# Decay exponents from running sums by head, and half of the xbc low parts by adding transfers

## The chip, the cores and the metric

The kernel runs on one core of one Trainium2 chip. The metric is device microseconds for one execution, the median of several runs. The program is written in Python against a tile framework: the framework allocates tiles from pools, sets the semaphores, and fixes one order of instructions for each engine when the program is built. The engines are PE (TensorE, matrix products into PSUM banks), DVE (VectorE), ACT (ScalarE), POOL (GpSimd) and SP (SyncE, which here only issues transfers). Each engine works through its own queue in order.

## The reference

One encoder block on 256 tokens of width 2048, all in float32. The part that matters here is the mixer:

```python
proj = rmsnorm(h, mix_norm_pre) @ w_in          # z (1024), xbc (1536), dt (32), u (1024)
xbc = silu(dwconv_centred(xbc, conv_w, conv_b)) # 5 taps over tokens
xs, bm, cm = split(xbc)                         # 16 heads of 64; 2 groups of state 128
dt = softplus(dt_raw + dt_bias); a = -exp(a_log)
# for each direction, chunk of 128 tokens and head:
acum  = cumsum(dt * a)
decay = exp(where(causal, acum[l] - acum[s], -inf))
y_diag = einsum(C B^T, decay, x * dt)           # + a term that crosses the chunks
```

Both directions run over the same tokens; the backward one is the forward one on flipped arrays. After the mixer come the pooling mixer, the shared output projection, a gated conv-MLP of width 5632 and a per-layer embedding. The change touches only `decay` and the way in which the xbc columns of `w_in` are prepared.

## The kernel before

**Products in two parts.** TensorE works on a rounded float32 form (called fp32r in the profile). To keep float32 accuracy the kernel splits every operand into a high part (rounded to that form) and a low part (the rest), and adds three products: high by high, high by low, low by high. `split` (lines 138 to 149) does this for weights: ACT copies 1024 columns into `...h` (L147), and DVE subtracts that from the source into `...l` (L148). The high and the low tiles rotate through five buffers each, the loaded slabs (`raw`, 1024 KB each, issued by SP) through three.

**Stages.** First the columns for dt and u (`dtu`, until 52.5 us), then three slabs of xbc (`xbc2`, `xbc0`, `xbc1` in this order, each 512 columns through `feature_major`), then z, then the output projection and the rest, which the change leaves alone. In `feature_major` (lines 268 to 283) a slab has four loads u; each load is split in two halves j, and each half feeds 24 matmuls of 256 columns. After a slab come the row scale (`xr`, L356), the convolution (ACT for the middle tap, L367, and 16 DVE instructions for the others, L373), and tanh and a product for silu.

**Work aside.** After every u, `aside()` takes the next list out of `work` and issues its jobs; so the attention-like work of the mixer lies between the xbc blocks. Which jobs stand in which list is written by hand (lines 623 to 656). The framework's own order may move a job's instructions a little among the neighbouring ones.

**The decays.** For each chunk t and group q of four heads (eight in all), `seg_prep` builds a 128 x 2048 page on POOL: the high and the low part of dt * a, each times a triangular mask, for both directions (four products, L509). `seg` then runs four matmuls of 512 columns against `m_gt` and `m_lt`, which add up the exponents over the steps between s and l for both directions in one PSUM bank, and ACT takes the exponential out of PSUM into `E` (L518). `weigh` multiplies `E` by C B^T and dt (POOL L581, DVE L586 and L590).

**Banks.** PSUM has six main banks and two `misc` banks. All the jobs aside (`pool_mix`, `decays`, `seg`, `pool_map`, `cb`, `xs_turn`, `mix`) take `misc` banks in turn, so a job's first matmul waits until the one two places earlier has been read out. `pool_map` is read out by ACT (`cath`, L183) and DVE (`catl`, L184).

Of the kernel before, what the change touches and what calls it, by code (L numbers as in the profile page):

```python
# [21 lines left out]
H = 16  # L22
# [29 lines left out]
def build(nc, a, out):  # L52
# [5 lines left out]
    with tile.TileContext(nc) as tc, \  # L58
# [8 lines left out]
        def ins(r):  # L67
            return getattr(r, "ins", r)

        def page(name, dtype=F32):  # L70
            return gp.tile([P, 2048], dtype, tag="pg", bufs=13, name=name)
# [10 lines left out]
        def misc(name):  # L82
            return pc.tile([P, 512], F32, tag="misc", name=name)

        def mm(o, lhsT, rhs, start, stop):
            nc.tensor.matmul(o, lhsT, rhs, start=start, stop=stop, skip_group_check=True)  # L86


        ep = early.enter_context(tc.tile_pool(name="early", bufs=1))
# [18 lines left out]

        xt = [ep.tile([P, V_SCW + L], F32, name="xt0")] + [page(f"xt{i}") for i in (1, 2)]
        vt = cp.tile([P, V_N - V_SCW], F32, name="vt")  # L110
        small = ep.tile([P, 80 + 512], F32, name="small")

        last = {}

# [12 lines left out]

        last["dma"] = load(xt[0], a["x_cols"][:, :V_SCW + L])
        dtb, alog, dsk = small[:, :32], small[:, 32:64], small[:, 64:80]
        mask = small[:, 80:].rearrange("p (m f) -> p m f", m=4)  # L130

        def vec(i):
            return xt[0][:, i:i + 1] if i < V_SCW else vt[:, i - V_SCW:i - V_SCW + 1]
# [2 lines left out]
        spare = {}  # L136

        def split(name, src, nel, cuts=()):

            if name in spare:  # L140
                hi, lo = spare.pop(name)
            else:
                hi = wp.tile([P, 1056], F32R, tag="whi", bufs=5, name=f"{name}h")
                lo = wp.tile([P, 1056], F32R, tag="wlo", bufs=5, name=f"{name}l")
            for c0, c1 in zip((0, *cuts), (*cuts, nel)):
                s = slice(c0, c1)
                last["act"] = ins(nc.scalar.copy(hi[:, s], src[:, s]))  # L147
                last["dve"] = ins(nc.vector.tensor_sub(lo[:, s], src[:, s], hi[:, s].bitcast(F32)))  # L148
            return hi, lo

        def raw(name, src, a_, b_):
# [116 lines left out]
        def feature_major(name, w, c0, get, acc):  # L268

            for u in range(4):  # L270
                r = raw(f"{name}r{u}", w[u * 512:(u + 1) * 512, c0:c0 + 512]
                        .rearrange("(k p) c -> p k c", p=P), 4, 512)
                for j in range(2):
                    wh, wl = split(f"{name}{u}_{j}", r[:, j * 1024:(j + 1) * 1024], 1024)
                    for kk in range(2):
                        k = 4 * u + 2 * j + kk
                        xh, xl = get(k)
                        for f in range(4):
                            s = slice(kk * 512 + f * P, kk * 512 + (f + 1) * P)
# [108 lines left out]
        for u in range(0, NK, 2):  # L388
            r = [wp.tile([P, 2048], F32, tag="raw", bufs=3, name=f"dtur{u}") if u else r0, page(f"dtur{u + 1}")]
            for j in range(2):  # L390
                k = u + j
# [35 lines left out]
        with tc.issue_after(half[0]), tc.issue_after(half[1]):  # L427
            xs_ = [page(f"x{t}") for t in range(2)]
            for t in range(2):
                load(xs_[t], x[t * P:(t + 1) * P, :])  # L430
            rx = row_rstd("rx", xs_)
            m_gt, m_lt = (ep.tile([P, P], F32R, name=n) for n in ("m_gt", "m_lt"))
            nc.vector.tensor_copy(m_gt, mask[:, 2, :])
            nc.vector.tensor_copy(m_lt, mask[:, 3, :])
            aneg = ep.tile([P, 32], F32, name="aneg")
            nc.scalar.activation(aneg, alog, AF.Exp)
            nc.gpsimd.tensor_scalar(aneg, aneg, -1.0, None, op0=ALU.mult)


            pt = page("pt")[:, :512].rearrange("p (k t) -> p k t", k=2)  # L440
            load(pt, a["p_t"])
            pth = cp.tile([P, 2, L], F32R, name="pth")
            ptl = cp.tile([P, 2, L], F32R, name="ptl")
            nc.scalar.copy(pth, pt)
            nc.vector.tensor_sub(ptl, pt, pth.bitcast(F32))
# [10 lines left out]
        for t in range(2):  # L456
# [3 lines left out]
                                    op0=ALU.mult)  # L460
# [17 lines left out]
        nc.vector.tensor_scalar(e3, e3, 2.0, None, op0=ALU.mult)  # L478
        nc.vector.scalar_tensor_tensor(dtf, dtf, 0.0, e3, op0=ALU.max, op1=ALU.add)
        da = ep.tile([P, 2, 32], F32, name="da")  # L480
        dah = ep.tile([P, 2, 32], F32R, name="dah")
        dal = ep.tile([P, 2, 32], F32, name="dal")
        nc.vector.tensor_tensor(da, dt, aneg.unsqueeze(1).to_broadcast([P, 2, 32]), op=ALU.mult)
        nc.vector.tensor_copy(dah, da)
        nc.vector.tensor_sub(dal, da, dah.bitcast(F32))

# [10 lines left out]
                nc.gpsimd.tensor_mul(dec[:, d, :], dec[:, d, :], dt[:, d, d * H:(d + 1) * H])  # L497


        ee = [page(f"E{t}") for t in range(2)]  # L500
        steps = {}

        def seg_prep(i):
            t, q = divmod(i, 4)
            ap_ = page(f"ap{i}", F32R).rearrange("p (a h l) -> p a h l", a=4, h=4)
            for j in range(4):
                d, src = j // 2, (dah.bitcast(F32), dal)[j % 2]
                hs = slice(d * H + 4 * q, d * H + 4 * q + 4)
                nc.gpsimd.tensor_tensor(ap_[:, j], src[:, t, hs].unsqueeze(2).to_broadcast([P, 4, P]),  # L509
                                        mask[:, d, :].unsqueeze(1).to_broadcast([P, 4, P]), op=ALU.mult)  # L510
            steps[i] = ap_

        def seg(i):
            t, q = divmod(i, 4)
            sps, ap_ = misc(f"seg{i}"), steps.pop(i)
            for j in range(4):
                mm(sps, (m_gt, m_lt)[j // 2], ap_[:, j].rearrange("p h l -> p (h l)"), j == 0, j == 3)
            nc.scalar.activation(ee[t][:, q * 512:(q + 1) * 512], sps, AF.Exp)  # L518


        cat = Panel.__new__(Panel)
# [97 lines left out]
        def job(f, *args):  # L619
            return lambda: f(*args)  # L620

        xd = {}
        work.extend([
            [job(seg_prep, 0)],
            [job(seg_prep, 1), job(pool_mix, 0), job(pool_mix, 1)],
            [job(seg_prep, 2), job(pool_mix, 2), job(pool_mix, 3), job(decays)],
            [job(seg_prep, 3), job(seg, 0)],
        ])
        bc = xbc(2)
        work.extend([  # L630
            [job(seg_prep, 4), job(seg, 1), job(pool_map, 0), job(pool_map, 1)],
            [job(seg_prep, 5), job(seg, 2), job(cb, bc, 0), job(cb, bc, 1)],
            [job(seg_prep, 6), job(seg, 3), job(pool_map, 2), job(pool_map, 3)],
            [job(seg_prep, 7), job(seg, 4), job(weigh, 0, 0)],
        ])
        xa = xbc(0)
        work.extend([
            [job(seg, 5), job(weigh, 0, 1)],
            [job(seg, 6), job(xs_turn, xa, 0)],
            [job(seg, 7), job(weigh, 1, 0)],  # L640
            [job(weigh, 1, 1)],
        ])
        xb = xbc(1)
# [21 lines left out]
        for t in range(2):  # L665
# [13 lines left out]
            r = rms(f"yn{t}", [ss], rz[t][:, 1:2], n=2)  # L679
# [65 lines left out]
        h = [page(f"h{t}") for t in range(2)]  # L745
# [118 lines left out]
        for half in range(2):  # L864
# [35 lines left out]
def laid_out(a):  # L900

    def cols(*vs):
        return np.concatenate([v.reshape(-1, P).T for v in vs], axis=1)

    return {
        "x_cols": np.concatenate([cols(a["mix_norm_pre"][0]),
                                  a["x"][0].T.reshape(NK, P, L).transpose(1, 0, 2).reshape(P, NK * L)], axis=1),
        "p_t": a["p"][0, 0].T.reshape(2, P, L).transpose(1, 0, 2),
        "columns": np.concatenate([
            cols(a["ssd_conv_w"][0], a["ssd_conv_b"][0], a["ssd_norm"][0], a["pool_scale"][0], a["ffn_norm_pre"][0],  # L910
                 a["ffn_conv_w"][0], a["ple_norm_pre"][0], a["ffn_conv_b"][0]),
            np.broadcast_to(np.concatenate([a[n][0].reshape(-1) for n in ("ssd_dt_bias", "ssd_a_log", "ssd_d")]),
                            (P, 80)),
            masks().transpose(1, 0, 2).reshape(P, 4 * P)], axis=1),
    }


def masks():
    j = np.arange(P)[:, None]
    l = np.arange(P)[None, :]  # L920
    return np.stack([j <= l, j >= l, j > l, j < l]).astype(np.float32)


def constants():
# [17 lines left out]
```

## Time and profile before

| | |
|---|---|
| median of 3 runs | 1146.65 us (1146.38 to 1147.10) |
| the profiled execution | 1147.28 us |
| its span | 1145.5 us |
| TensorE busy | 1126.3 us (98%) |
| VectorE, ScalarE, POOL busy | 824.8, 598.3, 122.5 us |
| granted TensorE clock, mean | 0.994 |

The profile comes from one execution. "Busy" is the time in which an engine had an instruction under way. The granted clock says what share of full speed TensorE was allowed; 1.00 is full. A chain is followed back from the last instruction, at each step to what released it. A wait names the engine and line that waited and the one whose end let it go. Rows that group instructions give the count, the busy time in all and the mean duration; rows of a timeline give the start, the length and the instruction. L numbers are lines of the kernel.

### The profile page before, as it was taken

Reading aid. Unit: us, or ns where it says so; the run is one execution under the profiler, and the core shown is the slowest. Engines: PE = TensorE matmul, PEld = TensorE weight load, DVE = VectorE, ACT = ScalarE, POOL = GpSimd, SP = SyncE. Lnnn points to the kernel's source line nnn. Section 1 sums busy time; section 2 is a strip of 40 time slices with the busy share of each in tenths; the row PEclk is TensorE's granted clock in tenths of the full one; section 3 lists DMA queues with packets and bytes.
Section 4 is the critical chain, followed back from the end, with each engine's and each line's share of the span. In section 5 each row is a group of like instructions: output and inputs, shape, how many; then the busy total and the mean of one; then the engine's idle time right before and its main releaser. Section 6 shows DMA issues by size and latency. Waiting matters only on the chain.

```text
span 1145.5 us, 15408 instructions
## 1 busy us (share of the span) xinstructions
PE 1126.3 (98%) x6057; PEld 971.6 (85%) x6057; DVE 824.8 (72%) x1060; ACT 598.3 (52%) x812; POOL 122.5 (11%) x123
## 2 busy tenths in 40 slices
PE   9998999999999999999999999999999999999996
PEld 9997987888888888888888888888888888887885
DVE  6578896654777665666766766668888888898573
ACT  7533543553675454544544545545555556657462
POOL 0274504200110000000000000000000000002001
PEclk9998999999999999999999999999999999999998
DMA  9952347546365555555555565556466646564752
GB/s 358 337 184 74 111 150 267 201 156 216 121 213 186 192 192 195 190 185 184 184 187 193 181 207 189 184 184 221 159 209 221 204 163 221 187 206 159 226 179 74
DMA packets 129592, 219.03 MB, mean 191 GB/s; under 512 B 3696, under 2 KB 96752, under 8 KB 128624
## 3 DMA queue, kind: packets, MB, share of 16 engines
q1 hardware_dynamic: 129232, 217.70, 57.4%
q8 instruction: 47, 0.77, 0.3%
q10 hardware_dynamic: 288, 0.36, 0.1%
q14 instruction: 25, 0.20, 0.1%
HBM read 215.95 MB, written 2.10 MB: 190 GB/s over the span
## 4 chain that ended last, share of the span: by engine, by line
PE 92%; DVE 5%; POOL 1%; ACT 1%; issue 1%; POOLq 0%; DVEq 0%; ACTq 0%
PE va L86 21%; PE ga L86 21%; PE dna L86 17%; PE woa L86 8%; PE gt L86 7%; PE dtu L86 4%; PE z L86 4%; PE xbc L86 3%; PE dns L86 3%; DVE cv L373 2%; DVE w L586 1%; DVE xb_0l L148 1%; PE ple L86 1%; PE yd L86 0%; DVE h L726 0%
## 5 line engine op out<-in xcount | busy, mean ns | idle before, releaser
L86 PE MATMUL ga<-wox,ug_0h 128*128 128x512 f32 x352 | 125.5, 395 | 0.0
L86 PE MATMUL ga<-wox,ug_1h 128*128 128x512 f32 x352 | 125.1, 394 | 0.0
L86 PE MATMUL va<-wox,uv_0h 128*128 128x512 f32 x352 | 124.8, 393 | 0.0
L86 PE MATMUL va<-wox,uv_1h 128*128 128x512 f32 x352 | 124.8, 393 | 0.0
L86 PE MATMUL ga<-wox,ug_0l 128*128 128x256 f32 x352 | 99.1, 282 | 0.0
L86 PE MATMUL ga<-wox,ug_1l 128*128 128x256 f32 x352 | 99.1, 282 | 0.0
L86 PE MATMUL va<-wox,uv_0l 128*128 128x256 f32 x352 | 99.1, 281 | 0.0
L86 PE MATMUL va<-wox,uv_1l 128*128 128x256 f32 x352 | 99.1, 281 | 0.0
L86 PEld LDWEIGHTS va<-wox,uv_0h 128*128 128x128 f32 x352 | 66.1, 188 | 15.0
L86 PEld LDWEIGHTS va<-wox,uv_1h 128*128 128x128 f32 x352 | 66.1, 188 | 15.0
L86 PEld LDWEIGHTS ga<-wox,ug_1h 128*128 128x128 f32 x352 | 66.1, 188 | 14.9
L86 PEld LDWEIGHTS ga<-wox,ug_0h 128*128 128x128 f32 x352 | 66.1, 188 | 14.8
L86 PE MATMUL dna<-dn_0h,hs 128*128 128x512 f32 x248 | 75.8, 393 | 0.0
L86 PE MATMUL dna<-dn_1h,hs 128*128 128x512 f32 x248 | 75.6, 393 | 0.0
L767 POOL TENSOR_TENSOR fc<-fc,rfb 128x1024 f32<-128x1024 f32 x11 | 26.4, 2404 | 440.2 <-ACT fc L766 440.2
L86 PEld LDWEIGHTS ga<-wox,ug_0l 128*128 128x128 f32 x352 | 66.2, 188 | 0.1
L86 PEld LDWEIGHTS ga<-wox,ug_1l 128*128 128x128 f32 x352 | 66.2, 188 | 0.0
L86 PEld LDWEIGHTS va<-wox,uv_0l 128*128 128x128 f32 x352 | 66.2, 188 | 0.0
L86 PEld LDWEIGHTS va<-wox,uv_1l 128*128 128x128 f32 x352 | 66.2, 188 | 0.0
L86 PEld LDWEIGHTS dna<-dn_1h,hs 128*128 128x128 f32 x248 | 46.5, 188 | 10.8
L86 PEld LDWEIGHTS dna<-dn_0h,hs 128*128 128x128 f32 x248 | 46.5, 188 | 10.7
L86 PE MATMUL dna<-dn_0l,hs 128*128 128x512 f32 x124 | 40.2, 393 | 0.0
(1075 smaller groups left out, 2860.3 us busy)
## 6 DMA issues: line engine op xcount, KB each, us to landing
dn0r<-w_ffn_down SPq DMA_DIRECT2D x22, 1024.0 KB, 5.5
dn1r<-w_ffn_down SPq DMA_DIRECT2D x22, 1024.0 KB, 5.5
zr<-w_in SPq DMA_DIRECT2D x8, 1024.0 KB, 5.2
wo0r<-w_out SPq DMA_DIRECT2D x8, 1024.0 KB, 5.6
wo1r<-w_out SPq DMA_DIRECT2D x8, 1024.0 KB, 5.5
gt0r<-w_ple_gate SPq DMA_DIRECT2D x8, 1024.0 KB, 6.0
gt1r<-w_ple_gate SPq DMA_DIRECT2D x8, 1024.0 KB, 5.6
dtur<-w_in SPq DMA_DIRECT2D x14, 528.0 KB, 8.6
```

Source lines behind the costliest of these rows:

```text
L86: nc.tensor.matmul(o, lhsT, rhs, start=start, stop=stop, skip_group_check=True)
L148: last["dve"] = ins(nc.vector.tensor_sub(lo[:, s], src[:, s], hi[:, s].bitcast(F32)))
L373: nc.vector.scalar_tensor_tensor(o[:, lo:hi], i[:, lo + d:hi + d], vec(wcol + j * wstep + f), o[:, lo:hi], op0=ALU.mult, op1=ALU.add)
L586: nc.vector.scalar_tensor_tensor(w[:, h * P:(h + 1) * P], cbm[:, 0, g, t, :], dt[:, t, 8 * g + h:8 * g + h + 1], w[:, h * P:(h + 1) * P], ...
L767: nc.gpsimd.tensor_tensor(cv.rearrange("p (f t) -> p f t", f=4), cv.rearrange("p (f t) -> p f t", f=4), rfb.unsqueeze(1).to_broadcast([P, ...
```

## The change

**Exponents.** `seg_prep` is gone. The new `seg_sums`, once, computes running sums by matmul: for each chunk and direction, `da4` (dt * a, four copies by head, the sign turned for the backward direction) against a mask gives c[l] for all 16 heads in 64 rows, 16 heads in four blocks. It splits c into high and low, and spreads it by ACT over two pages: `seg_x` holds c[l] in rows 0 to 31 (high, low) and selectors in rows 32 to 63; `seg_w` holds negated selectors and c[s] so that a single matmul over 64 rows gives c[l] - c[s] for four heads. The selector halves are filled earlier, in the dtu stage (eight ACT instructions). `seg` is now one matmul of 512 columns for each direction, into two `misc` banks; ACT copies the first out, DVE takes the minimum with the second (the direction in which the pair is causal has the smaller exponent), and ACT takes the exponential in place.

**Low parts.** In `feature_major` the second half (j = 1) of each load now goes through `split_far`: ACT writes the negated slab, rounded, to the low tile; POOL issues a transfer that reads the same 512 KB of `w_in` from device memory again and adds it to that tile; ACT writes the high tile. So DVE has no part in it. There are 12 of these.

**Order.** The jobs aside are dealt anew: `seg_sums` goes into the third list, `seg` runs from the fourth on (two at first, then one each), and `cb` moves two lists later. The constants of `small` grow by nine columns.

```diff
+        low, among, four = small[:64, 592:593], small[:64, 593:597], small[:64, 597:601]
...
+        def split_far(name, src, far, nel):
...
+            nc.scalar.activation(lo[:, :nel], src[:, :nel], AF.Copy, scale=-1.0)
+            o = lo[:, :nel]
+            if len(far.shape) == 3:
+                o = o.rearrange("p (k c) -> p k c", k=far.shape[1])
+            nc.gpsimd.dma_start(o, far, accum_op=ALU.add)
+            nc.scalar.copy(hi[:, :nel], src[:, :nel])
+            return hi, lo
...
-                    wh, wl = split(f"{name}{u}_{j}", r[:, j * 1024:(j + 1) * 1024], 1024)
+                    piece = r[:, j * 1024:(j + 1) * 1024]
+                    if j:
+                        wh, wl = split_far(f"{name}{u}_{j}", piece, w[u * 512 + 256:(u + 1) * 512, c0:c0 + 512]
+                                           .rearrange("(k p) c -> p k c", p=P), 1024)
+                    else:
+                        wh, wl = split(f"{name}{u}_{j}", piece, 1024)
...
-            m_gt, m_lt = (ep.tile([P, P], F32R, name=n) for n in ("m_gt", "m_lt"))
-            nc.vector.tensor_copy(m_gt, mask[:, 2, :])
-            nc.vector.tensor_copy(m_lt, mask[:, 3, :])
+            seg_w = page("seg_w", F32R)[:64, :].rearrange("p (a q s) -> p a q s", a=4, q=4)
+            seg_x = page("seg_x", F32R)[:64, :].rearrange("p (a i l) -> p a i l", a=4, i=4)
+            for a_ in range(4):
+                nc.scalar.activation(seg_w[:32, a_], four[:32].unsqueeze(2).to_broadcast([32, 4, P]), AF.Copy,
+                                     scale=-1.0)
+                nc.scalar.copy(seg_x[32:, a_], among[32:].unsqueeze(2).to_broadcast([32, 4, P]))
...
-        dah = ep.tile([P, 2, 32], F32R, name="dah")
-        dal = ep.tile([P, 2, 32], F32, name="dal")
+        da4 = ep.tile([P, 2, 2, 4, H], F32, name="da4")
...
-        nc.vector.tensor_copy(dah, da)
-        nc.vector.tensor_sub(dal, da, dah.bitcast(F32))
+        for d in range(2):
+            nc.vector.tensor_scalar(da4[:, :, d], da[:, :, d * H:(d + 1) * H].unsqueeze(2).to_broadcast([P, 2, 4, H]),
+                                    1.0 - 2.0 * d, None, op0=ALU.mult)
...
-        def seg_prep(i):
...
-                nc.gpsimd.tensor_tensor(ap_[:, j], src[:, t, hs].unsqueeze(2).to_broadcast([P, 4, P]),
-                                        mask[:, d, :].unsqueeze(1).to_broadcast([P, 4, P]), op=ALU.mult)
+        def seg_sums():
+            cps = misc("cps")
+            for a_ in range(4):
+                mm(cps[:64, a_ * P:(a_ + 1) * P], da4[:, a_ // 2, a_ % 2].rearrange("p r h -> p (r h)"),
+                   mask[:, 3 * (a_ % 2), :], True, True)
+            hi, c = page("seg_h", F32R)[:64, :512], page("seg_c")[:64, :512]
+            nc.scalar.copy(hi, cps[:64, :])
+            nc.vector.scalar_tensor_tensor(c, hi.bitcast(F32), low, cps[:64, :], op0=ALU.mult, op1=ALU.add)
+            c4 = c.rearrange("p (a l) -> p a l", a=4)
+            for i in range(4):
+                nc.scalar.activation(seg_x[:32, :, i, :], c4[:32], AF.Copy, scale=among[:32, i:i + 1])
+                nc.scalar.activation(seg_w[32:, :, i, :], c4[32:], AF.Copy, scale=four[32:, i:i + 1])
...
         def seg(i):
             t, q = divmod(i, 4)
-            sps, ap_ = misc(f"seg{i}"), steps.pop(i)
-            for j in range(4):
-                mm(sps, (m_gt, m_lt)[j // 2], ap_[:, j].rearrange("p h l -> p (h l)"), j == 0, j == 3)
-            nc.scalar.activation(ee[t][:, q * 512:(q + 1) * 512], sps, AF.Exp)
+            ps = [misc(f"seg{i}{d}") for d in range(2)]
+            for d in range(2):
+                mm(ps[d], seg_w[:, 2 * t + d, q], seg_x[:, 2 * t + d].rearrange("p i l -> p (i l)"), True, True)
+            e = ee[t][:, q * 512:(q + 1) * 512]
+            nc.scalar.copy(e, ps[0])
+            nc.vector.tensor_tensor(e, ps[1], e, op=ALU.min)
+            nc.scalar.activation(e, e, AF.Exp)
...
         work.extend([
-            [job(seg_prep, 0)],
-            [job(seg_prep, 1), job(pool_mix, 0), job(pool_mix, 1)],
-            [job(seg_prep, 2), job(pool_mix, 2), job(pool_mix, 3), job(decays)],
-            [job(seg_prep, 3), job(seg, 0)],
+            [],
+            [job(pool_mix, 0), job(pool_mix, 1)],
+            [job(pool_mix, 2), job(pool_mix, 3), job(decays), job(seg_sums)],
+            [job(seg, 0), job(seg, 1)],
         ])
         bc = xbc(2)
         work.extend([
-            [job(seg_prep, 4), job(seg, 1), job(pool_map, 0), job(pool_map, 1)],
-            [job(seg_prep, 5), job(seg, 2), job(cb, bc, 0), job(cb, bc, 1)],
-            [job(seg_prep, 6), job(seg, 3), job(pool_map, 2), job(pool_map, 3)],
-            [job(seg_prep, 7), job(seg, 4), job(weigh, 0, 0)],
+            [job(seg, 2), job(pool_map, 0), job(pool_map, 1)],
+            [job(seg, 3), job(pool_map, 2), job(pool_map, 3)],
+            [job(cb, bc, 0), job(cb, bc, 1), job(seg, 4)],
+            [job(seg, 5), job(weigh, 0, 0)],
         ])
         xa = xbc(0)
         work.extend([
-            [job(seg, 5), job(weigh, 0, 1)],
-            [job(seg, 6), job(xs_turn, xa, 0)],
-            [job(seg, 7), job(weigh, 1, 0)],
+            [job(seg, 6), job(weigh, 0, 1)],
+            [job(seg, 7), job(xs_turn, xa, 0)],
+            [job(weigh, 1, 0)],
             [job(weigh, 1, 1)],
         ])
```

More of the change, by code (lines that the diff above doesn't have):

```diff
@@ L110, in build @@
         vt = cp.tile([P, V_N - V_SCW], F32, name="vt")
-        small = ep.tile([P, 80 + 512], F32, name="small")
+        small = ep.tile([P, 89 + 512], F32, name="small")
         last = {}
@@ L129, in build @@
         dtb, alog, dsk = small[:, :32], small[:, 32:64], small[:, 64:80]
-        mask = small[:, 80:].rearrange("p (m f) -> p m f", m=4)
+        mask = small[:, 80:592].rearrange("p (m f) -> p m f", m=4)
+        low, among, four = small[:64, 592:593], small[:64, 593:597], small[:64, 597:601]
         def vec(i):
@@ L148, in split @@
                 last["dve"] = ins(nc.vector.tensor_sub(lo[:, s], src[:, s], hi[:, s].bitcast(F32)))
+            return hi, lo
+        def split_far(name, src, far, nel):
+            if name in spare:
+                hi, lo = spare.pop(name)
+            else:
+                hi = wp.tile([P, 1056], F32R, tag="whi", bufs=5, name=f"{name}h")
+                lo = wp.tile([P, 1056], F32R, tag="wlo", bufs=5, name=f"{name}l")
+            nc.scalar.activation(lo[:, :nel], src[:, :nel], AF.Copy, scale=-1.0)
[4 more added lines that the diff above has]
+            nc.scalar.copy(hi[:, :nel], src[:, :nel])
             return hi, lo
@@ L273, in feature_major @@
                 for j in range(2):
-                    wh, wl = split(f"{name}{u}_{j}", r[:, j * 1024:(j + 1) * 1024], 1024)
+                    piece = r[:, j * 1024:(j + 1) * 1024]
+                    if j:
+                        wh, wl = split_far(f"{name}{u}_{j}", piece, w[u * 512 + 256:(u + 1) * 512, c0:c0 + 512]
+                                           .rearrange("(k p) c -> p k c", p=P), 1024)
+                    else:
+                        wh, wl = split(f"{name}{u}_{j}", piece, 1024)
                     for kk in range(2):
@@ L500, in build @@
         ee = [page(f"E{t}") for t in range(2)]
-        steps = {}
-        def seg_prep(i):
-            t, q = divmod(i, 4)
-            ap_ = page(f"ap{i}", F32R).rearrange("p (a h l) -> p a h l", a=4, h=4)
-            for j in range(4):
-                d, src = j // 2, (dah.bitcast(F32), dal)[j % 2]
-                hs = slice(d * H + 4 * q, d * H + 4 * q + 4)
-                nc.gpsimd.tensor_tensor(ap_[:, j], src[:, t, hs].unsqueeze(2).to_broadcast([P, 4, P]),
-                                        mask[:, d, :].unsqueeze(1).to_broadcast([P, 4, P]), op=ALU.mult)
-            steps[i] = ap_
+        def seg_sums():
[10 more added lines that the diff above has]
+                nc.scalar.activation(seg_w[32:, :, i, :], c4[32:], AF.Copy, scale=four[32:, i:i + 1])
         def seg(i):
             t, q = divmod(i, 4)
-            sps, ap_ = misc(f"seg{i}"), steps.pop(i)
-            for j in range(4):
-                mm(sps, (m_gt, m_lt)[j // 2], ap_[:, j].rearrange("p h l -> p (h l)"), j == 0, j == 3)
-            nc.scalar.activation(ee[t][:, q * 512:(q + 1) * 512], sps, AF.Exp)
+            ps = [misc(f"seg{i}{d}") for d in range(2)]
[5 more added lines that the diff above has]
+            nc.scalar.activation(e, e, AF.Exp)
         cat = Panel.__new__(Panel)
@@ L913, in laid_out @@
                             (P, 80)),
-            masks().transpose(1, 0, 2).reshape(P, 4 * P)], axis=1),
+            masks().transpose(1, 0, 2).reshape(P, 4 * P), head_rows()], axis=1),
     }
@@ L921, in masks, with head_rows @@
     return np.stack([j <= l, j >= l, j > l, j < l]).astype(np.float32)
+def head_rows():
+    p = np.arange(P)[:, None]
+    i = np.arange(4)[None, :]
+    return np.concatenate([-((p // 16) % 2), p % 4 == i, -1.0 * (p % 16 // 4 == i)], axis=1).astype(np.float32)
 def constants():
```

## The prediction

> **What bounds the kernel now.** I read the share of each engine first, then the waits of TensorE in the stretch that the change touches, then the chain that ended last there.
>
> ```profile
> span 1145.5 us, 15408 instructions
> PE 1126.3 (98%) x6057; PEld 971.6 (85%) x6057; DVE 824.8 (72%) x1060; ACT 598.3 (52%) x812; POOL 122.5 (11%) x123
> ```
>
> TensorE is busy nearly all the time, so the program gets shorter by TensorE work that goes, by TensorE waits that go, and by time at a lower clock. The profiled execution took 1147.28 us (span 1145.5 and 1.8 around it), 0.63 above the median 1146.65. The waits of TensorE from 50 to 245 us (in all, times, longest), and the chain in that stretch (start, length, what):
>
> ```profile
> PE seg L86 <- DVE catl L184: 4.9, 1, 4.9
> PE dps L86 <- DVE mixt L532: 0.6, 1, 0.6
> PE xbc L86 <- DVE xb_0l L148: 0.5, 1, 0.5
> ```
> ```profile
> 52.77 11.41 PE xbc L86 x96
> 64.18 1.86 PE mx L86 x16
> ...
> 75.30 1.06 PE dps L86 x8
> ...
> 102.74 2.04 PE seg L86 x4
> 104.78 3.41 PE cb L86 x8
> 108.20 5.84 PE xbc L86 x48
> 114.04 0.93 PE seg L86 x4
> 114.96 3.45 PE pw L86 x16
> 118.42 5.71 PE xbc L86 x48
> ...
> 152.48 22.22 PE z L86 x96
> 174.70 0.87 PE xt L564 x8
> ```
>
> From the first xbc matmul at 52.77 to the first z matmul at 152.48 are 99.7 us. Its work at full clock: 576 xbc matmuls at 11.41/96 = 0.119 are 68.5; mx twice 1.86, 3.7; dps 1.1; eight seg of 0.93, 7.4; pw twice 3.45, 6.9; cb, eight records at pw's 3.45/16 = 0.216, 1.7; xt 0.9. Together 90.2. The waits above are 6.0. The work behind the long wait is slow: seg 2.04 in place of 0.93, cb 3.41 in place of 1.7, the 48 xbc 0.1 more, 2.9 in all. That leaves 0.6 unassigned. The clock (last but two columns) shows why, and the DVE and POOL orders show what the long wait stood behind:
>
> ```profile
> 98.00:100.00 2.00, 0.00 (x0) 0.00 (x0) 2.00 (x3) 1.65 (x3) 0.00 (x0) 1.00 0.02 4
> 102.00:104.00 2.00, 1.26 (x3) 1.10 (x4) 1.45 (x3) 2.00 (x4) 0.00 (x0) 0.50 0.72 279
> 52.77:152.48 99.71, 93.64 (x697) 89.62 (x697) 83.10 (x138) 43.55 (x62) 49.83 (x38) 0.97 0.35 116
> ```
> ```profile
> 83.53 14.24 DVE L373 SCALAR_TENSOR_TENSOR cv<-xr,vt,cv 128x254 f32<-128x254 f32 x16
> 126.39 6.39 DVE L373 SCALAR_TENSOR_TENSOR cv<-xr,vt,cv 128x254 f32<-128x254 f32 x16
> ```
> ```profile
> 94.69 1.22 POOL L509 TENSOR_TENSOR ap<-dal,small 128x512 fp32r<-128x512 f32 x1
> 123.02 2.02 POOL L509 TENSOR_TENSOR ap<-dal,small 128x512 fp32r<-128x512 f32 x1
> ```
>
> The same 16 taps took 14.24 us while POOL ran seg_prep (to 95.9) and 6.39 just after its last one (125.0). In the first case the catl of pool_map stood behind the taps, and TensorE stood for a PSUM bank behind catl.
>
> **The change part by part.** Rows for the prices (busy us and mean ns behind the bar; the last three are from timelines):
>
> ```profile
> L509 POOL TENSOR_TENSOR ap<-dal,small 128x512 fp32r<-128x512 f32 x16 | 22.4, 1399 | 0.0
> L509 POOL TENSOR_TENSOR ap<-dah,small 128x512 fp32r<-128x512 f32 x16 | 19.3, 1208 | 26.6 <-DVE dah L484 20.7 <-PE seg L86 5.9
> L581 POOL TENSOR_TENSOR w<-cbm,dt 128x1024 f32<-128x1024 f32 x4 | 8.5, 2120 | 23.8 <-DVE cbm L556 11.3 <-DVE cv L373 7.9 <-DVE E L590 3.0
> L148 DVE TENSOR_TENSOR xb_1l<-xb1r,xb_1h 128x1024 fp32r<-128x1024 f32 x4 | 5.5, 1366 | 1.9 <-ACT xb_1h L147 1.9
> L356 DVE TENSOR_TENSOR xr<-xbc,rxb 128x512 f32<-128x512 f32 x4 | 2.6, 680 | 0.0
> L586 DVE SCALAR_TENSOR_TENSOR w<-cbm,dt,w 128x128 f32<-128x128 f32 x32 | 12.1, 446 | 1.8 <-POOL w L581 1.8
> L590 DVE TENSOR_TENSOR E<-E,w 128x1024 f32<-128x1024 f32 x3 | 3.6, 1215 | 0.0
> L518 ACT ACTIVATE E<-seg 128x512 f32<-128x512 f32 x8 | 4.7, 593 | 0.5 <-PE seg L86 0.5
> L147 ACT CAST xb_1h<-xb1r 128x1024 fp32r<-128x1024 f32 x4 | 4.2, 1051 | 3.2 <-PE xbc L86 3.2
> ```
> ```profile
> 40.78 1.05 ACT L147 CAST xb_0h<-xb2r 128x1024 fp32r<-128x1024 f32 x1
> 82.96 1.58 ACT L367 ACTIVATE cv<-xr,vt 128x256 f32<-128x256 f32 x3
> ```
> ```profile
> 109.53 2.18 DVE L586 SCALAR_TENSOR_TENSOR w<-cbm,dt,w 128x128 f32<-128x128 f32 x8
> ```
>
> *TensorE.* Of each seg's four 512-column matmuls two stay: 16 at 22.22/96 = 0.231 are 3.7 in place of 7.4. No row shows a matmul over 64 rows; the rows go by columns (256 take 0.119, 512 take 0.231), so I take 0.231; at half of it 1.9 more would go, at double the seg gain is lost (both kept for the range). seg_sums adds four fp32 matmuls of 128 columns: mx has eight of 136 in 1.86, so 0.9. Work falls from 90.2 to 87.4.
>
> *POOL.* The 32 seg_prep products (41.7 us) go, 12 transfer issues come. I take the taps of the first conv at 6.4 in place of 14.2.
>
> *DVE.* Twelve subtractions of 1024 go (1.37 each, 16), and four small copies (m_gt, m_lt, dah, dal); eight minima of 512 out of PSUM (0.68 as xr, 5.4), seg_c (0.7) and two small da4 products come.
>
> *ACT.* Twelve negated copies at 1.05 (12.6), eight plain copies of seg (4.7), seg_h 0.6, and 16 fills of 512 columns at 0.5 to 0.6 (8 to 9; three cv of 256 took 1.58, so about 0.53 apart). Within the 99.7 us ACT goes from 43.6 to some 66: it still has room. The first eight fills stand before xb_0h, which started at 40.78; it moves to 44.8 and is needed at 52.77, so they cost nothing; without that cover they would cost 4.
>
> *SP.* The x loads, pmat and poolw keep their order; the second xbc load goes ahead of pt, pmat and poolw, and the third has the same loads ahead of it as before. pmat is needed by mx at 64.2, poolw by pool_map at 91 in the walk below, and the full queue ends near 53: nothing late.
>
> *Two misc banks.* A seg now takes both, so each seg and each pool_map waits for the copy and the minimum of the one before. Walking the four queues in the order in which the changed program has them, with these durations: seg_sums' matmuls end near 77.7, seg_c at 79.1, the fills at 84.4 (behind one cast), and the first seg comes at 84.5: covered by about 0.5. TensorE then waits 0.4 for the copy of seg 2 ahead of pool_map 0, 0.25 and 0.5 for the catl of pool_map 0 and 1 ahead of seg 3 (the third minimum stands behind all taps, at 94.1), 0.2 ahead of pool_map 2, 0.3 ahead of the transposes of xs, and 0.6 for dps as before: 2.3 in all, none of it long. With no long wait the 2.9 of slow clock go too. Then z starts at 52.77 + 87.4 + 2.3 + the 0.6 left over = 143.1, which is 9.4 earlier.
>
> *What is late next.* DVE. After the second conv (ends 126.8 in the walk) it has two minima, a split, the 1024-wide cv product, 24 of the w taps at 0.27 to 0.45, three E products of 1.2, two z splits, xr and z2_0l; they end at 146.5. Then come the taps of the third conv (6.4), and behind these z2_1l, ready at 154.0; TensorE, started on z at 143.1, wants it at 152.4. I charge 1.7. It was no wait before, because DVE stood 9 us further ahead of z.
>
> *The add transfers.* No row shows a transfer issued by POOL, or one that adds. Nearest:
>
> ```profile
> xb0r<-w_in SPq DMA_DIRECT2D x4, 1024.0 KB, 5.0
> xb2r<-w_in SPq DMA_DIRECT2D x4, 1024.0 KB, 10.6
> ```
> ```profile
> DMA packets 4912, 9.74 MB, mean 361 GB/s; under 512 B 179, under 2 KB 2227, under 8 KB 4653
> ```
>
> The third row is the stretch 28 to 55 us, where the queue is full: 1024 KB at 361 GB/s are 2.9, so 2.1 of the 5.0 do not go with size, and a plain 512 KB would land in 3.6. If the add moves the bytes twice it is 5.0, and with one POOL instruction of about 1.2 to write the issue 6.2: I take 6. The upper end is 10.6, the loads in the full queue. What it may take, by the walk, from issue to the matmul that needs it: 8.4, 11, 11, 16, 15, **6.2**, 9.8, 15, 12, 10, 12, **7.4** us. The sixth is issued at 89.8, since its negation stands on ACT behind the fills, two seg copies and four cv; the twelfth at 132.6, because on POOL it stands behind the w products of weigh (2.1 each), which wait for the second conv's taps and cv product. At 6 nothing waits; at 8, 2.4; at 10, 8.2; at 11, 13.2; at 12, 20.
>
> The Trainium skill, page "DMA: Bandwidth & Descriptors", section "Anatomy of one DMA", puts a POOL-issued transfer at 2.0 us plus its bytes at 436 GB/s; by it 512 KB would land in an estimated 3.2 and the sum stays as it is. No run here shows it, and it prices no add. The page "SBUF — State Buffer" of the Trainium skill (section "Who interferes with whom") says that VectorE instructions in a two-port mode (copies, tensor_scalar) lock POOL out of writing descriptors. By it almost nothing here would block, for the DVE work at the issues is tensor_tensor and taps; a lock wider than it says is the third rival.
>
> *Sum.* 1147.28 - 9.4 + 1.7 = 1139.6; against the median 1139.0. I say 1139.5.
>
> **The rivals.**
> *The adds land late* (the other side). Place: the third matmul of each second half-slab. For it: no row of such a transfer; raw loads share the queues, and ACT, then POOL, delays issues. Against: the stretch moves 116 GB/s, far from 361. Break-even: the waits must eat 9.4 (the z2_1l wait goes as DVE catches up), which is a landing of about 10.3. At 11, 1147.28 - 9.4 + 13.2 = 1151; at 12, 1158.
> *The taps stay slow.* If not POOL but something else made them 14.2, the third minimum comes 7.9 later, pool_map 1 waits about 7 and the clock falls again: -9.4 + 7 + 2.9 = 1147.8, no change. Against: the two rows of 16 taps.
> *POOL cannot write while DVE works.* The sixth transfer then starts when the taps end at 93.4 and lands at 99.4, 3.4 after its need: 1143.
> *Better.* DVE keeps ahead of z (the w taps at 0.27, 2.2 for eight), and the small waits are covered: 1147.28 - 9.4 - 2.3 = 1135.6.
>
> **How the numbers follow.** Forecast, 1137.5 to 1142: 0.50. Better: 0.12. Locked POOL or longer bank waits, to 1144.3: 0.12. Slow taps, or adds near 9 to 10: 0.09. Late adds: 0.17. A measurement tells about 0.2% (1144.4 to 1148.9 is no change), so faster 0.74, same 0.09, slower 0.17. The range goes from below the better case, with part of the half-price seg, to adds landing at 11: 1134.5 to 1150.5; the forecast's own is 1137.5 to 1142.
>
> **What would show it.** Right: 16 taps near 6.4 in the first conv; no TensorE wait over 1 us and clock 1.00 from 80 to 140; z starting near 143; POOL issues landing in 5 to 7; a wait of z for z_1l of 1 to 3 us near 152. Wrong: xbc matmuls waiting for a transfer by POOL, two seg matmuls well over 0.46, or DVE still full from 80 to 100 with taps of 0.85.

## The result, and the profile after

The changed kernel takes 1152.78 us (median; 1151.99 to 1155.68), the kernel before 1146.66 in the same comparison: a ratio of 1.0058, 95% interval 1.0039 to 1.0076. It got slower by half a per cent, where 1139.5 was forecast and 1150.5 was the upper end of the range. The profiled execution took 1151.99 (span 1150.2 and 1.8 around it), 4.7 more than the profiled one before. Its engines, from the first part of the page:

```profile
span 1150.2 us, 15424 instructions
PE 1128.4 (98%) x6049; PEld 969.9 (84%) x6049; DVE 806.2 (70%) x1055; ACT 624.6 (54%) x849; POOL 94.8 (8%) x103
```

TensorE's waits from 40 to 260 us in the changed kernel (in all, times, longest), and three stations of its TensorE timeline (start, length, what, idle before and its releaser):

```profile
PE xbc L86 <- DMA xb_1l<-w_in: 3.9, 2, 2.4
PE z L86 <- DVE z_1l L150: 3.0, 1, 3.0
PE z L86 <- DVE z_0l L150: 0.8, 1, 0.8
PE seg L86 <- ACT seg_x L541: 0.7, 1, 0.7
```
```profile
149.68 0.63 PE L86 MATMUL z<-z_0h,hnh 128*128 128x512 f32 x2
...
163.19 1.22 PE L86 MATMUL z<-z_1l,hnh 128*128 128x512 f32 x2 [2.97 <-DVE z_1l L150]
...
177.70 1.03 PE L598 MATMUL xt<-ident,cv 128*128 128x128 f32 x8
```

The long wait for catl (4.9) is gone, as forecast. In its place stand waits for adding transfers ahead of z, and waits for VectorE inside z. By starts in the timeline, four stretches tell the rest:

| stretch | before | after | difference |
|---|---|---|---|
| up to the first z matmul | 152.32 | 149.68 | -2.6 |
| from there to the transposes of xs | 22.2 | 28.0 | +5.8 |
| from there to the first gate matmul | 868.0 | 867.8 | -0.2 |
| the gate stage, 900 us later | 90.5 | 92.1 | +1.6 |

They add up to 4.6 of the 4.7. The clock (last but two columns) gives what the waits don't: behind the wait of 3.0 it fell to a half, and it did so again in the gate stage, whose code is the same. The first two rows are z and the third is the gate stage of the changed kernel; the row in the second fence is the kernel before behind its wait in the gate stage:

```profile
164.00:166.00 2.00, 2.00 (x6) 1.52 (x6) 2.00 (x3) 0.00 (x0) 0.00 (x0) 0.50 0.77 205
166.00:168.00 2.00, 2.00 (x10) 1.59 (x9) 2.00 (x3) 0.00 (x0) 0.00 (x0) 0.90 1.05 360
...
1052.00:1054.00 2.00, 2.00 (x10) 1.87 (x9) 0.82 (x2) 0.47 (x1) 0.00 (x0) 0.54 0.97 299
```
```profile
1048.00:1050.00 2.00, 2.00 (x15) 1.74 (x14) 1.93 (x4) 0.99 (x3) 0.00 (x0) 1.00 0.55 127
```

So z lost 3.8 to waits and about 2.0 to the clock. The gate stage is luck: after an equal wait of 2.2 for `gt_1l` the kernel before kept its clock (the last row), and over the fourteen profiles of this case that stage took 90.5 to 90.6 in six and 91.9 to 92.1 in eight, whatever had been changed. The first and last matmuls of one group of that stage, before and after:

```profile
L86 PE MATMUL gt<-gt_0h,dnxh x56: 277/392/502, 1042.5 to 1133.0; 128*128 128x512 f32 x50, 128*128 128x256 f32 x6
```
```profile
L86 PE MATMUL gt<-gt_0h,dnxh x56: 278/392/498, 1045.5 to 1137.6; 128*128 128x512 f32 x50, 128*128 128x256 f32 x6
```

What was forecast right can be seen on VectorE. The sixteen taps of the first conv, with the second of the minima of `seg` between them, and later the taps of `w` beside POOL's products and without them:

```profile
89.44 1.77 DVE L395 SCALAR_TENSOR_TENSOR cv<-xr,vt,cv 128x254 f32<-128x254 f32 x4
91.12 0.69 DVE L551 TENSOR_TENSOR E<-seg,E 128x512 f32<-128x512 f32 x1
91.72 4.81 DVE L395 SCALAR_TENSOR_TENSOR cv<-xr,vt,cv 128x255 f32<-128x255 f32 x12
...
137.28 5.60 DVE L620 SCALAR_TENSOR_TENSOR w<-cbm,dt,w 128x128 f32<-128x128 f32 x7
...
144.54 2.44 DVE L620 SCALAR_TENSOR_TENSOR w<-cbm,dt,w 128x128 f32<-128x128 f32 x9
...
155.60 6.40 DVE L395 SCALAR_TENSOR_TENSOR cv<-xr,vt,cv 128x254 f32<-128x254 f32 x16
161.91 1.22 DVE L150 TENSOR_TENSOR z_1l<-zr,z_1h 128x1024 fp32r<-128x1024 f32 x1
```

The taps of the first conv take 6.6 (4 and 12) in place of 14.24, now that POOL has no `seg_prep`. The last two rows are the wait of 3.0: `z_1l` stands on VectorE behind the sixteen taps of the third conv.

Two prices were new. The transfers (median from issue to landing, last column), and a visit of seg among the xbc matmuls, first of one, then of two:

```profile
xb_1l<-w_in POOLq DMA_DIRECT2D x12, 512.0 KB, 8.7
```
```profile
88.82 0.28 PE L86 MATMUL xbc<-hnh,xb_1l 128*128 128x256 f32 x1
89.03 0.50 PE L86 MATMUL seg<-seg_x,seg_w 64*128 64x512 f32 x1
89.46 0.38 PE L86 MATMUL xbc<-hnh,xb_1h 128*128 128x256 f32 x1
89.68 0.28 PE L86 MATMUL xbc<-hnl,xb_1h 128*128 128x256 f32 x1
...
92.56 0.28 PE L86 MATMUL xbc<-hnh,xb_1l 128*128 128x256 f32 x1
92.77 0.73 PE L86 MATMUL seg<-seg_x,seg_w 64*128 64x512 f32 x2
93.43 0.38 PE L86 MATMUL xbc<-hnh,xb_0h 128*128 128x256 f32 x1
93.65 0.28 PE L86 MATMUL xbc<-hnl,xb_0h 128*128 128x256 f32 x1
```

Read by starts: xbc matmuls follow each other at 0.12. From 88.82 to 89.68 are 0.86, of which two steps of 0.12 belong to xbc, so the one seg cost 0.62; from 92.56 to 93.65 are 1.09, so two cost 0.85. By 0.231 each they would be 0.23 and 0.46. The sixteen matmuls come in five such pairs (the first of them behind a wait, taken at the price of the others) and six single visits: 5 x 0.85 + 6 x 0.62 = 8.0 us, in place of the 3.7 reckoned, and more than the 7.4 of before.

### The profile page after: what moved, and what is told of

Same layout as the page of the kernel before. It is cut to its first block, busy times and chain, and to the rows that moved or that the text cites. A ratio compares the mean times of both kernels' runs of the same rounds, so it can differ in the third digit from the quotient of the medians.

```text
span 1150.2 us, 15424 instructions
## 1 busy us (share of the span) xinstructions
PE 1128.4 (98%) x6049; PEld 969.9 (84%) x6049; DVE 806.2 (70%) x1055; ACT 624.6 (54%) x849; POOL 94.8 (8%) x103
## 4 chain that ended last, share of the span: by engine, by line
PE 88%; DVE 5%; issue 2%; DMA 2%; ACT 2%; POOL 1%; DVEq 0%; POOLq 0%; ACTq 0%
PE va L86 21%; PE ga L86 21%; PE dna L86 17%; PE woa L86 8%; PE gt L86 7%; PE z L86 3%; PE dns L86 3%; PE dtu L86 3%; PE xbc L86 2%; DMA xb_1l<-w_in 2%; DVE cv L395 1%; DVE w L620 1%; PE ple L86 1%; PE yd L86 0%; DVE E L624 0%
## 5 line engine op out<-in xcount | busy, mean ns | idle before, releaser
L86 PEld LDWEIGHTS dna<-dn_0h,hs 128*128 128x128 f32 x248 | 46.5, 188 | 10.7
```

## The experiments

The twelve runs share the kernel before as their measure; its medians there were 1146.8 to 1147.2, against 1146.66 in the comparison of the result. So a difference between two runs that is well under a microsecond tells nothing. "The changed kernel" is 1152.8.

**1. Seg on 128 rows.**

```
-seg_w = page("seg_w", F32R)[:64, :]...      (seg_x alike)
+seg_w = page("seg_w", F32R)...
+for o in (seg_w, seg_x): for a_ in range(4):
+    nc.gpsimd.tensor_scalar(o[64:, a_]..., mask[64:]..., 0.0, None, op0=ALU.mult)
```

> The changed kernel with the two operands of seg widened from 64 to 128 rows; rows 64 to 127 are zeros, written once on POOL before they are needed, so the sums are the same. Theory one, 'the row count has a price': in the changed kernel a visit of two seg matmuls to the stream of xbc matmuls costs 0.85 us and of one 0.62, where two times 0.231 and 0.231 were reckoned; 0.4 of each is the change from 128-row to 64-row matmuls and back. Then here two cost about 0.46 to 0.5 and one 0.23 to 0.27, the eleven visits give back 4.2 us, z starts near 145.5 in place of 149.7, and the time falls by 2.5 to 4 (VectorE then decides at z). Theory two, 'a seg matmul is dear for another reason' (two PSUM banks, new weights): the visits stay at 0.85 and 0.62 and z starts at 149.7.

Measured: 1157.09 (ratio 1.0082, 1.0067 to 1.0097). The price is as theory one has it, in the same places of the TensorE timeline:

```profile
97.67 0.28 PE L86 MATMUL xbc<-hnh,xb_1l 128*128 128x256 f32 x1
97.79 0.63 PE L86 MATMUL seg<-seg_x,seg_w 128*128 128x512 f32 x2
98.26 0.28 PE L86 MATMUL xbc<-hnh,xb_0h 128*128 128x256 f32 x1
98.37 0.27 PE L86 MATMUL xbc<-hnl,xb_0h 128*128 128x256 f32 x1
...
109.75 0.28 PE L86 MATMUL xbc<-hnh,xb_0l 128*128 128x256 f32 x1
109.87 0.40 PE L86 MATMUL seg<-seg_x,seg_w 128*128 128x512 f32 x1
110.11 0.28 PE L86 MATMUL xbc<-hnh,xb_0h 128*128 128x256 f32 x1
```

A pair costs 0.46 and a single one 0.24 (two of the six single visits cost 0.4), with the same banks and columns. The difference is 0.38 to 0.39 whether a visit has one matmul or two: so it was the change between 64 and 128 rows that cost this, once a visit. The time went the other way because the zeros took POOL 12 us between 38.8 and 52.3, and the first two adding transfers were issued from 53.8 on in place of 48.6 and 51.4: TensorE waited 6.6 for transfers, and the clock fell (0.50 from 62 to 66).

**2. The exponents alone.**

```
-if j: wh, wl = split_far(...)
-else: wh, wl = split(f"{name}{u}_{j}", piece, 1024)
+wh, wl = split(f"{name}{u}_{j}", piece, 1024)
```

> The changed kernel with all low parts of xbc by subtraction on VectorE again: only the exponents are changed against the kernel before. Theory one, 'the late transfers cost': the waits of 2.4 and 1.4 for transfers go, VectorE's twelve subtractions (1.2 each) hide, and the time is 3 to 4 below the changed kernel. Theory two, 'VectorE decides at z': VectorE, full from 116 to 164 in the changed kernel, gets six of the twelve subtractions back in that stretch, z waits up to 7 us longer for its low parts, and the time is up to 4 above the changed kernel.

Measured: 1152.91 (1.0044, 1.0029 to 1.0059), the same as with the transfers. The time lies between the two theories: no wait for a transfer is left, but one for VectorE is 5.2, and the clock behind it is low. What the twelve transfers cost TensorE, they save about as much on VectorE. This run differs in one thing more: the framework put the first z matmuls ahead of the last xbc matmuls (they start at 137.8), as also in runs 8 and 12 (135.2 and 137.4). No run separates this order from the missing transfers.

```profile
PE z L86 <- DVE z_0l L150: 5.2, 1, 5.2
PE xbc L86 <- DVE xb_1l L150: 2.4, 1, 2.4
```

**3. The transfers alone** (the kernel before with `split_far` in `feature_major`, the exponents by `seg_prep`).

> The kernel before with the twelve adding transfers alone; the exponents stay as before, with their 32 products on POOL. If a late landing costs what it did in the changed kernel (8 to 11 us from issue), and the issues stand on POOL's queue behind products of 1.2 to 2 us, several of the twelve come late and the time is 5 to 20 us above the kernel before. If the transfers are hidden and the relief of VectorE counts, it is 2 to 5 below it.

Measured: 1149.74 (1.0021, 1.0012 to 1.0030), below what lateness was to cost, and for another reason. TensorE waited 0.9 for transfers, but 5.7 for `mixt`, which stood on VectorE behind this subtraction; the POOL rows are the first and the last of the eight products beside it:

```profile
66.42 1.33 DVE L148 TENSOR_TENSOR xb_0l<-xb0r,xb_0h 128x1024 fp32r<-128x1024 f32 x1 [3.67 <-ACT xb_0h L147]
...
73.99 6.91 DVE L148 TENSOR_TENSOR xb_0l<-xb0r,xb_0h 128x1024 fp32r<-128x1024 f32 x1 [5.04 <-ACT xb_0h L147]
```
```profile
71.38 1.49 POOL L529 TENSOR_TENSOR ap<-dah,small 128x512 fp32r<-128x512 f32 x1
...
78.37 1.44 POOL L529 TENSOR_TENSOR ap<-dal,small 128x512 fp32r<-128x512 f32 x1
```

The same instruction took 1.33 and, beside POOL's unbroken run of products, 6.91. But it isn't always VectorE that waits. Beside the subtraction of 1.33 a product of POOL took 2.02, and in the first conv of this run the sixteen taps kept their 6.39 while a product beside them took 5.61; the wait for catl is not there:

```profile
95.22 6.39 DVE L393 SCALAR_TENSOR_TENSOR cv<-xr,vt,cv 128x254 f32<-128x254 f32 x16
```
```profile
98.04 5.61 POOL L529 TENSOR_TENSOR ap<-dah,small 128x512 fp32r<-128x512 f32 x1 [0.40 <-PE seg L86]
```

What decides which of the two engines waits was not tested.

**4. The same transfers without adding.**

```
-nc.gpsimd.dma_start(o, far, accum_op=ALU.add)
+nc.gpsimd.dma_start(o, far)
```

> The changed kernel with the same twelve transfers, same bytes and same places, that overwrite their target and do not add (the low parts of half of xbc are then the raw weights, so the output is another). Theory one, 'the adding is what makes them slow' (bytes moved twice): the median from issue to landing falls from 8.7 to 4 to 6 us, the waits of xbc for them go, z starts 3 to 4 earlier. Theory two, 'a POOL issue beside the raw loads is slow whatever it does': the median stays at 8 to 9 and the waits stay.

Measured: 1146.40 (0.9989, 0.9979 to 0.9998), 6.4 below the changed kernel. Theory one holds: from issue to landing the median is 6.1 (just above its 4 to 6), no xbc matmul waits for a transfer, and z starts near 145.8. In the profiled executions 3.9 of the gain are these waits. Another 1.8 are in z, where the wait for `z_1l` is 3.0 as before but the clock stayed at 1.00 behind it. POOL's queue took 1.8% of the DMA engines' span where it had taken 3.1% for the same bytes; the rows are those of this run's transfers and queue, then the queue of the changed kernel:

```profile
xb_1l<-w_in POOLq DMA_DIRECT2D x12, 512.0 KB, 6.1
```
```profile
q0 software_dynamic: 3264, 6.29, 1.8%
```
```profile
q0 software_dynamic: 3264, 6.29, 3.1%
```

**5. Seg on 128 rows, the zeros by VectorE** (as in 1, with two `nc.vector.tensor_scalar` over 64 x 2048).

> The changed kernel with the operands of seg on 128 rows again, the zeros now written by two instructions on VectorE near 40 us, where it is idle, so that POOL's first transfers keep their places. The first try cost no more per matmul than a 128-row one but moved POOL. Theory one (the row count has a price of 4.2 us in the visits): z starts 3 to 4.5 earlier than 149.7, the second conv 2 to 3 earlier, and the time is 2 to 4 below the changed kernel (1149 to 1151). Theory two (the earlier arrival only turns into longer waits for the transfers, whose landing does not move): the two waits of xbc grow by what seg saves and the time stays within 1 of the changed kernel.

Measured: 1152.21 (1.0049, 1.0034 to 1.0064), 0.6 below the changed kernel: theory two. The 4.2 us of TensorE work are gone, yet z starts at 150.1. The zeros delayed the first xbc matmul by 0.6 (53.02, not 52.43), the waits up to z grew by 1.7, to 6.3, and behind the first of them, 2.4 long as in the changed kernel, the clock fell here and cost 1.6. Together 3.9; some 0.7 is not assigned.

**6. Both repairs** (4 and 5 together).

> Both repairs at once: transfers that overwrite (the low parts of half of xbc are then the raw weights, so the output is another) and 128-row seg. If the prediction failed only in these two terms, z starts near its 143.1, z waits 1.5 to 3 for z_1l, and the time is 1139 to 1142. If VectorE's work ahead of z (the E products, 24 taps of w, the third conv) was undersized as well, z starts near 142 but waits 5 or more, the clock falls, and the time is 1143 to 1146.

Measured: 1145.10 (0.9987, 0.9977 to 0.9996). z starts at 143.8, against the forecast's 143.1. But it waits:

```profile
PE z L86 <- DVE z_1l L150: 3.0, 1, 3.0
PE z L86 <- DVE z_0l L150: 1.5, 1, 1.5
PE xt L602 <- DVE cv L613: 1.0, 1, 1.0
```

So the walk up to z fell on these two terms, and a third one was undersized: VectorE's work ahead of z. Its waits in z, 4.5, come near the 5 of the second theory, though the clock stayed at 1.00 behind them.

**7. The third conv behind the second block of z.**

```
-xb = xbc(1)
+xb_acc, xb = xbc(1, False), []            (the matmuls alone)
 work.extend([[],
-             [],
+             [lambda: xb.append(silu(1, xb_acc))],   (row scale, taps, tanh, product)
              [], [job(xs_turn, ...)], ...
```

> The changed kernel with the third conv's row scale, taps and product moved behind the second block of z, so that on VectorE the low parts of the first z blocks stand ahead of the 16 taps (6.4 us); all else in its order. Theory one (z waits because VectorE does the taps first): the wait of 3.0 for z_1l goes, with the slow clock behind it (2), and the time is 3 to 5 below the changed kernel (1148 to 1150). Theory two (the waits only move to the transposes of xs, which need that conv): no change within 1.

Measured: 1147.70 (1.0010, 1.0001 to 1.0019), 5.1 below the changed kernel, by the place of the third conv alone. The waits in z shrank from 3.8 to 1.0 and the clock stayed at 1.00 there; the two waits for transfers are as they were.

```profile
PE xbc L86 <- DMA xb_1l<-w_in: 3.5, 2, 2.4
...
PE z L86 <- DVE z_0l L150: 0.8, 1, 0.8
...
PE z L86 <- DVE z_1l L150: 0.2, 1, 0.2
```

**8. No transfers, 128 rows, the later conv** (2, 5 and 7 together).

> The exponents by running sums without the adding transfers, 128-row seg, and the third conv behind the second block of z. If the price of 64 rows (4.2), the landing of the transfers and the taps ahead of z are what ate the gain, this one is the fastest: z starts near 143, and the time is 1139 to 1144, below the kernel before. If VectorE is the bound from 116 on whatever the order, it stays at 1147 to 1150.

Measured: 1146.04 (0.9991, 0.9981 to 1.0000), between the theories: z no longer waits, but an xbc matmul waits 4.2 for a low part on VectorE, which has the twelve subtractions back, and the clock falls behind it (0.79 on average from 132 to 148, some 3 us lost).

**9, 10, 11. Four, eight and all twelve transfers**, with 128 rows and the later conv. The edit of 9; in 10 the condition is `name != "xb2"`, in 11 there is none:

```
-if j:
+if j and name == "xb1":
     wh, wl = split_far(...)
```

> The exponents by running sums on 128-row operands, the third conv behind the second block of z, and the adding transfers in the last slab of xbc alone (four of twelve), where in the changed kernel they landed in 5.7 to 8.9 us and nothing waited for them; the other two slabs split on VectorE. If the transfers are bad only where they land late, VectorE's four subtractions go from its full stretch, the wait of 4.2 for a low part in the version without transfers goes, and the time is 4 to 7 below that version's 1146.0 (1139 to 1142, z near 143). If the transfers cost wherever they are, it is 1146 or more.

> As the run with four transfers, but with eight: in the second and third slab of xbc. The sixth of the changed kernel's transfers (second slab, issued at 93 behind ScalarE's fills, landed 8.5 later) is among them. By the theory of late landings TensorE waits 1 to 3 us for it here, and the time is 1 to 3 above the run with four.

> The changed kernel with all twelve transfers, 128-row seg and the later third conv. By the theory of late landings the second and the sixth transfer cost 4.5 us of waiting and perhaps a slow clock behind it, so 4 to 7 above the run with four; seg on 128 rows gives at most 2 against the same with 64 rows (1147.7), because VectorE decides. If landing late costs nothing once z no longer waits, it equals the run with four.

Measured: 1142.23 (0.9956, 0.9939 to 0.9973), 1145.18 (0.9983, 0.9974 to 0.9992) and 1148.60 (1.0017, 1.0007 to 1.0026). With run 8 at no transfers this is one series: 1146.0, 1142.2, 1145.2, 1148.6 (between the first two the order of TensorE changes as well, see run 2). Where they land in time they pay. The sixth costs a wait of 2.1 in run 10, where the clock stayed at 1.00. The first (the expectation says the second) and the sixth cost 4.6 in run 11, and there the clock falls to 0.5 for some microseconds behind each. Run 9 beats both kernels, though it stays just above its forecast of 1139 to 1142. Its z starts at 143.2, and its waits are:

```profile
PE z L86 <- DVE z_0l L150: 1.9, 1, 1.9
PE xt L602 <- DVE cv L616: 1.1, 1, 1.1
```

**12. No transfers, 64 rows, the later conv** (2 and 7).

> The version without transfers and with the later third conv, but with 64-row seg: the price of 64 rows where no transfer is waited for. If TensorE is the bound there, it is 3 to 4 above the 1146.0 of the same with 128 rows; if VectorE is, 0 to 1.5.

Measured: 1145.58 (0.9988, 0.9979 to 0.9998), not above the 1146.04 of run 8. So also here the 4.2 us of TensorE work buy nothing. In run 8, which is without them, TensorE comes to the same low part earlier and waits 4.2 for it, and the clock falls; here it waits 2.4, and the clock stays at 1.00 from 132 to 148. VectorE decides when z can go on.

## Why the prediction was wrong

Against the sum of 1139.6 the profiled execution is 12.4 late: 6.8 at the start of z (2.6 earlier than before, where 9.4 was forecast), 4.1 in z (5.8 against 1.7) and 1.6 in the gate stage; the stretch between gives 0.2 back, and 0.1 lies outside the four.

- **The long wait: right.** "I take the taps of the first conv at 6.4": 6.6. The wait for catl went, and the clock is 1.00 from 80 to 140. The rival of slow taps falls: in run 2, without `seg_prep` and without transfers, they also take 6.6. Run 3 narrows the cause. POOL's products can stretch VectorE's work (a subtraction there), but in that run the taps took 6.39 beside one; so a product beside the taps need not slow them, and why the products of the kernel before did so was not tested further.
- **The price of seg: wrong, the step "Of each seg's four 512-column matmuls two stay: 16 at ... 0.231 are 3.7".** They cost 8.0 in their places, 4.3 more; even the upper end that was kept, double, is passed. It was priced by columns, from rows in which nothing changes from one matmul to the next; the price lies in the change, which a row count of 64 among 128 brings twice a visit (shown by runs 1 and 5). The Trainium skill, page "TensorEngine Tiling (Array Packing)", section "Key Properties", says that changing the tiling mode drains TensorE, without a figure. The traces agree in that a visit with another row count costs 0.38 to 0.39 us more; that it is a drain they don't show. It was the rule that spoke against the change, and the prediction missed it.
- **The landing: wrong in size, the step "I take 6".** Median 8.7, from 5.7 to 10.7. The mechanism was right: by the walk a landing of 8.7 costs 4.1, and TensorE waited 3.9. In part this is luck, for it waited for the first (2.4) and the sixth (1.4), where the walk had the sixth and the twelfth as the tightest; the twelfth landed in 5.7. The estimate let the add move the bytes twice beside an empty queue; plain transfers among the raw loads already take 6.1, and adding 2.6 more (run 4), of which 0.5 is POOL's own instruction (1.19 against 0.72). The sixth was issued at 93.1, not 89.8: the eight fills on ACT began some 2 us late, behind the wait for the first transfer, and took 0.72 each and not 0.53.
- **The waits for two misc banks: too many.** Of the 2.3 charged, only 0.7 (the fills) appeared. That took 1.6 off the errors above: 4.3 + 3.9 - 1.6 is 6.6 of the 6.8.
- **What is late next: the right engine, the wrong size, the step "I charge 1.7".** VectorE's taps ahead of `z_1l` were named, and run 7 shows them to be the cause. But the second conv ended at 132.8, not 126.8, since the slab ahead of it was late, and from there to `z_1l` VectorE needed 30 us where the walk had 27: seven taps of `w` beside POOL's products took 0.80 each (the prediction had at most 0.45), and a subtraction beside them took 2.56 where it had 1.37. The clock, which lost another 2.0 behind the wait, was in no term for z. In run 6, with the other two repaired, the waits in z are still 4.5.
- **The gate stage: not in the prediction.** 1.6 of the 12.4 are a clock that fell there or not.
- **The rivals.** "The adds land late" named the place but set its point at a landing of 10.3; the sign changed at 8.7, because its 3.9 came on top of two other errors. "POOL cannot write while DVE works" falls: the sixth issue stands at 93.14, 0.3 after its negation, in the midst of the taps. Of the three wrong terms, the landing (8.7, with 10.6 as the upper end) and the wait for `z_1l` (3.0, with 1 to 3 expected) stood within their bounds and seg just beyond (8.0 against 7.4 at double price); that three fail to the same side was given no case.

The terms don't add as times. TensorE's 4.2 for seg can be given back with little gain or none (run 5 against the changed kernel 0.6, run 6 against run 4 1.3; runs 8 against 12 and 11 against 7 none), while 5.1 come from the place of the third conv and 6.4 from the landing, 1.8 of it the clock in z. Three things stay open: why adding takes a transfer that much longer beyond POOL's instruction and the DMA engines' share, what decides whether the clock falls, and which of POOL and VectorE waits where they meet.

## What to carry to other kernels

A small matmul of another shape among large ones is priced by a pair of starts around it, not by its columns; zero rows up to the common shape made a visit cheaper, though here the time hardly followed. A transfer that adds beside other loads needs, by the landings here (5.7 to 10.7), an issue 9 to 11 us ahead of its need, and is used only where that much time is there: here for four of twelve. When a wait goes, look on every engine for what now stands in front of the next stage: here the place of sixteen taps was worth 5.1 us.

## What the runs showed of the hardware

**Behind a wait of 2.2 to 3.0 us the clock sometimes halved and sometimes didn't.** The same wait for the first transfer, 2.4 long at the same place, in the changed kernel and in run 5 (the rows are the stretch behind it):

```profile
59.00:61.00 2.00, 2.00 (x19) 2.00 (x18) 0.47 (x3) 0.00 (x0) 0.00 (x1) 1.00 1.10 262
```
```profile
59.00:61.00 2.00, 2.00 (x10) 2.00 (x11) 0.98 (x5) 0.00 (x0) 0.59 (x1) 0.50 1.09 261
```

A fall behind such a wait lasted some 4 us and cost 1.6 to 2.0; behind the wait of 3.0 for `z_1l` the clock fell in the changed kernel and stayed at 1.00 in runs 4 and 6. The Trainium skill, page "TensorE: Matmul & The Clock Gate", section "Why this matters for your kernels", advises to keep idle gaps under about 3 us; here the clock also fell behind gaps of 2.2 to 2.4, so a shorter gap was no protection.

**POOL's products and VectorE's two-input work stretched each other**, VectorE's by up to five times (6.91 against 1.33 for one subtraction, 0.80 against 0.27 for a tap of `w`), and in run 3 a product of POOL to 5.61 beside taps that kept their time. **The adding cost a transfer 1.7 times the DMA engines' time** (3.1% against 1.8% of the span).
